# A fourth block of the up projection through seven products, with its sums, transposes and combinations moved

## The chip, the cores and the metric

The kernel runs on one core of one Trainium2 chip. The metric is the device time of one execution in microseconds (us), the median of several runs. Lower is better. Inputs, weights and the result are float32 in the chip's main memory, and the products must hold nearly float32 accuracy.

## The reference

One residual block over 256 tokens of width 2048: a mixer (retention and latent attention, merged by gates, then `w_out`), and behind it an MLP with a squared ReLU. The change lies in the last two lines of the loop and in the seam to them.

```python
def reference(x, ...):
    h = x
    u = _rmsnorm(h, norm_mix_g[l])
    h = h + _mixer(u, ...)                      # ends in merged @ w_out
    z = _rmsnorm(h, norm_mlp_g[l]) @ w_up[l]    # (256 x 2048) @ (2048 x 8192)
    h = h + jnp.square(jax.nn.relu(z)) @ w_down[l]
    return _rmsnorm(h, norm_f_g)
```

## The kernel before, in words

**Splitting.** Every float32 operand is split into two parts, `hi` (ScalarE casts, L550) and `lo` (VectorE subtracts, L551), and a product of two operands is three matmuls: hi by hi, hi by lo, lo by hi. So each weight tile of 128 x 1024 that a DMA brings into a `raw` buffer costs one ScalarE cast and one VectorE subtraction before TensorE can use it. There are five `raw` buffers, and seven pairs of `hi` and `lo` in this stage (four, and three named `more`).

**The MLP's up projection** has 8192 columns. It is computed in two ways.

- *Units* (`Unit`, L1264): 128 columns at a time, in two halves of 8 contraction tiles. A half is 8 matmuls of 512 columns (the weight's `hi` against both parts of the tokens, L176) and 8 of 256 columns (`lo`, L180), into one PSUM bank `z`. At the end ScalarE copies the bank out (L1291), VectorE adds its two halves (L1292), ScalarE applies ReLU and the square, and GpSimd's queue stores the result to the array `hid`.
- *Steps* (`Step`, L287): 1024 columns, a *block*, at a time, as a 2 x 2 block product with seven block products in place of eight. A block takes eight steps, one for each 256 rows of the contraction. A step is four parts with 2, 2, 2 and 1 products, 21 matmuls of 512 columns (L333 to L335) into seven PSUM banks `zs`, one for each product. Of the chip's eight banks one is left for `z` or for transposes. A step's weights come by two DMAs of 512 KB (`sraw` and `raw`), and VectorE forms their sums `forms` (L307, L316, L317) before these are split like other weights.

The tokens' side of the seven products needs combinations of token blocks, `hc` (`combine`, L221). One call of `make` makes those of a quarter of the contraction, that is of two steps, and holds two `raw` buffers while it does.

When a block's last step is done, `s_end` (L515) combines the seven banks into the block's four quarters in the tile `zo`. These have tokens in the partitions, but the down projection wants columns there, so four *turns* (`turn`, L1302) transpose them on TensorE, four 128 x 128 transposes each into a bank `zt`, and ScalarE squares and GpSimd stores.

**The order** in this stage is written by hand. `stream` (L470) walks a list of *parts* (a part of a step, or half a unit). At part n it issues the loads up to part n+6, the preparation (split, sums) up to part n+4, then the matmuls of part n; then `soon` (L463) issues what was put in the list `later` with a delay counted in parts. The instructions of each engine run in just this order, and each engine waits in place.

In the list stand three early units, then the blocks with units between their parts, then two late units. Before the change there are three blocks and 40 units. 35 units stand inside: one behind the last part of each step but the last, and one behind the second part of every other step. A turn stands ahead of the second part of steps 1 to 4 of the next block; the last block's turns stand with the late units.

```python
            for f, i, o in PRODUCTS:               # L329
                if i == part:
                    ...
                    PE.matmul(q, ah, hi[:, o], start=first, stop=False)
                    PE.matmul(q, al, hi[:, o], start=False, stop=False)
                    PE.matmul(q, ah, lo[:, o], start=False, stop=last)
```

**The seam.** Ahead of the stage, `wo` (the product with `w_out`, L1233) runs over four column blocks, with tokens transposed (L1224) one block later. The first two quarters of `hc` are made beside its second and third column blocks; quarters three and four are made in the stage, from parts 7 and 24 on, a piece every second part. Behind the stage, the down projection `dn` (L357 to L359) reads `hid` back and uses products of the same two kinds; it is not edited, but takes the pairs of columns in the order of units first, then blocks.

Of the kernel before, what the change touches and what calls it, by code (L numbers as in the profile page):

```python
# [13 lines left out]
F32R = mybir.dt.float32r  # L14
# [3 lines left out]
ALU = mybir.AluOpType  # L18

P = 128  # L20
S = 256
D = 2048
KT = D // P
# [4 lines left out]
CHUNK = 64  # L28
DFF = 8192
FT = DFF // P  # L30
SU = 3
SJ = KT // 2
ST = SU * 1024 // P
EARLY, LATE = 3, 2
AHEAD = 4
PAIRED = 6
# [69 lines left out]
def block_kernel(ctx: ExitStack, tc: tile.TileContext, A):  # L106
# [9 lines left out]
    def big(name, dt=F32, shape=(P, KT, S)):  # L116
        return act.tile(list(shape), dt, tag="act16", name=name)
# [127 lines left out]
    class Combos:  # L245
# [4 lines left out]
            self.name, self.pair, self.t = name, pair, []  # L250

        def make(self, c):
            if c % 2 == 0:
                self.t.append(big(f"{self.name}{c // 2}", F32R, (P, KT // 4, 2, 4, P)))
            return combine(self.pair, 2 * c, self.t[-1][:, c % 2 * 2 : c % 2 * 2 + 2])

        def get(self, f, j):
# [29 lines left out]
    class Step:  # L287
# [32 lines left out]
            pass  # L320

        def mm(self, part):
            if part == 0 and self.j == 0:
                self.qs.update({f: (mmps if f in (3, 4, 2, 5) else atps)(f"zs{uid[0]}{f}") for f in (3, 4, 2, 5, 6, 1, 7)})
            if part == 1:
                self.between()
            hi, lo = self.ws.pop(part)
            first, last = self.j == 0, self.j == SJ - 1
            for f, i, o in PRODUCTS:  # L329
                if i == part:  # L330
                    ah, al = self.x.get(f, self.j)
                    q = self.qs[f]
# [3 lines that stand above are left out]
            if part == 3 and last:  # L336
                self.end()
# [123 lines left out]
    later = []  # L461
# [5 lines left out]
                later.remove(entry)  # L467
                entry[1]()

    def stream(parts, after):  # L470
        loaded = prepped = 0
        for n, (it, h) in enumerate(parts):
            ahead = AHEAD if n else 2
            while loaded < min(len(parts), n + ahead + 3):
# [37 lines left out]
            st.after = last  # L512
        return parts

    def s_end(qs, out, tmp):  # L515
# [3 lines left out]
        def tt(eng, o, a, b, op=ALU.add):  # L519
            eng.tensor_tensor(out=o, in0=a, in1=b, op=op)  # L520

        SC.copy(t3, qs[3])
        tt(V, e, qs[6], t3)
        SC.copy(q5, qs[5])
        tt(V, f, qs[2], e, ALU.subtract)
        SC.copy(c12, qs[1])
        tt(V, c21, qs[4], f)
        SC.copy(c22, qs[7])
        tt(V, c11, q5, f)
        yield  # L530
        tt(V, e, e, q5, ALU.subtract)
        yield
        tt(V, c12, c12, e)
        yield
        tt(V, c22, c22, t3)
        yield

    def join(out, ps):
# [689 lines left out]
                split(hT.hi(kt), hT.lo(kt), pT[:, j * S : (j + 1) * S], scale=g)  # L1228
    zp = ctx.enter_context(tc.tile_pool(name="zp", bufs=1))
    hidd = ctx.enter_context(tc.tile_pool(name="hidd", bufs=1, space=bass.MemoryType.DRAM))  # L1230
    hc = Combos("hc", hT)
# [32 lines left out]
    class Unit:  # L1264
# [23 lines left out]
        def evict(self):  # L1288
            pair, n = divmod(ST + self.i, 2)
            t = zp.tile([P, 2, S], F32, tag="hs", bufs=5, name=f"hs{pair}{n}")  # L1290
            SC.copy(t, self.ps.rearrange("p (j n) -> p j n", j=2))  # L1291
            V.tensor_tensor(out=t[:, 0], in0=t[:, 0], in1=t[:, 1], op=ALU.add)  # L1292
# [18 lines left out]

    def step(u, j, qs):
        def end():
            sums = s_end(qs, zo[:, 0].rearrange("p (t c) n -> p t c n", t=2), zo[:, 1])
# [19 lines left out]
    slots = [(u, j, h) for u in range(SU) for j in range(SJ) for h in (1, 3)][:-1]  # L1334
    whole = [t for t in slots if t[2] == 3]
    room = len(units) - len(whole)
    halves = [t for t in slots if t[2] == 1]
    if room >= 0:
        use = set(whole) | {halves[i * len(halves) // room] for i in range(room)}
    else:  # L1340
        use = {t for t in whole if t[1] != PAIRED or t[0] >= -room}
    for u in range(SU):
        qs = {}
        for j in range(SJ):
# [8 lines left out]
        un = Unit(i, 0, drain(((0, 1), (1, 2))[n]))  # L1353
        parts += [(un, 0), (un, 1)]

    hp = ctx.enter_context(tc.tile_pool(name="hp", bufs=1))
    combs, sets = {}, {}
    ssf = cp.tile([P, 2, SSF], F32, name="ssf")
    rf = cp.tile([P, 2], F32, name="rf")
# [126 lines left out]
    def after(n):  # L1486
        nonlocal making, zo, keep, hn2, gt
        if n == 0:
            mlp_turn(3)
            keep = hidd.tile([P, 2, D], F32, name="hnkeep")  # L1490
            SC.dma_start(keep, hn)
            zo = big("zo", shape=(P, 2, 4, 512))
        elif n in MAKE:
            making = hc.make(2 + MAKE.index(n))
        if n < 2 * EARLY or n % 2 == 0:
            next(making, None)
        if hooks.get(n) == 0:
# [4 lines left out]
        elif hooks.get(n) == 1:  # L1502
            for t in range(2):
                for c in range(2):
# [3 lines left out]
                    later.append([2 * t + c, one])  # L1508
                    later.append([6 + 2 * t + c, lambda t=t, c=c: scale(t, c)])

    zo = keep = hn2 = gt = None
    rings(zp, MORE, True, forms)
    with tc.manual_schedule(engines=MANUAL):
        stream(parts, after)
        assert not later
        for t in range(2):
            for c in range(2):
# [98 lines left out]
```

## Time and profile before

| What | Value |
|---|---|
| median of 3 runs | 1564.05 us (1563.8 to 1564.08) |
| the profiled execution | 1564.87 us |
| its span, first to last instruction | 1563.1 us |
| granted TensorE clock, mean | 0.998 |
| up projection, first `z` to first `dn` matmul | 876 to 1221 us |
| down projection | 1221 to 1563 us |

The page of the profile gives for each engine the time in which it was busy. PE is TensorE with its matmuls, PEld its weight loads, DVE VectorE, ACT ScalarE, POOL GpSimd, SP the engine whose queue issues the loads. A matmul's duration in the rows is its latency; matmuls are pipelined, and one follows the other sooner than that. What a stretch of work takes is therefore read from starts, or from the chain of waits, in which each piece stands with the time that the path spent in it.

### The profile page before, as it was taken

The numbers are of one execution on the slowest core, as the hardware profiler recorded it, in microseconds if no ns is written. First come the engines' busy times: TensorE is split into PE (matmuls) and PEld (weight loads), VectorE is DVE, ScalarE is ACT, GpSimd is POOL, SyncE is SP. The second block draws the span as 40 slices with busy tenths as digits, with TensorE's granted clock in tenths as the row PEclk, the third lists the DMA queues.
The fourth block names the chain that finished last, engine by engine and source line by source line (L and its number), as shares of the span: only waits on it lengthen the run. The fifth ranks groups of instructions, "written<-read, shape, count | busy, mean of one in ns | idle before, by whom it ended". The sixth has DMA issues, their size and how long they took to land.

```text
span 1563.1 us, 21388 instructions
## 1 busy us (share of the span) xinstructions
PE 1550.3 (99%) x7655; PEld 1310.8 (84%) x7655; DVE 1317.3 (84%) x1787; ACT 962.8 (62%) x1416; POOL 39.1 (3%) x76
## 2 busy tenths in 40 slices
PE   9999999999999999999999999999999999999997
PEld 7888888888898888888888888888888888888886
DVE  7998877899977988976566698887978899989996
ACT  7546555566545667874445566676767766656664
POOL 0000000000000000000000000000000100000000
PEclk9999999999999999999999999999999999999999
DMA  8666755466656664445556657676675977686773
GB/s 328 208 202 208 234 163 160 154 202 211 203 170 222 207 197 149 158 127 164 191 197 217 234 193 252 210 229 229 212 247 190 375 269 240 235 308 210 265 256 115
DMA packets 107626, 333.70 MB, mean 213 GB/s; under 512 B 11264, under 2 KB 12160, under 8 KB 106496
## 3 DMA queue, kind: packets, MB, share of 16 engines
q1 hardware_dynamic: 104208, 318.71, 61.3%
q0 software_dynamic: 3168, 11.54, 1.8%
q10 hardware_dynamic: 144, 2.10, 0.4%
q8 instruction: 60, 0.98, 0.2%
q14 instruction: 46, 0.38, 0.1%
HBM read 319.72 MB, written 12.58 MB: 213 GB/s over the span
## 4 chain that ended last, share of the span: by engine, by line
PE 78%; DVE 2%; issue 1%; ACT 1%; DMA 0%; DVEq 0%; POOLq 0%; POOL 0%; ACTq 0%
PE z L176 9%; PE dn L359 7%; PE dn L358 7%; PE dn L357 7%; PE z L180 5%; PE zs L335 2%; PE zs L333 2%; PE zs L334 2%; PE mo L214 2%; PE mo L215 2%; PE mo L217 2%; PE wo L214 2%; PE wo L215 2%; PE wo L217 2%; PE gm L357 2%; PE yr L358 2%
## 5 line engine op out<-in xcount | busy, mean ns | idle before, releaser
L169 DVE TENSOR_TENSOR lo<-raw,hi 128x1024 fp32r<-128x1024 f32 (+1 forms) x148 | 173.2, 1172 | 90.9 <-ACT hi L168 90.8
L551 DVE TENSOR_TENSOR lo<-raw,hi 128x1024 fp32r<-128x1024 f32 (+3 forms) x214 | 232.1, 1101 | 20.1 <-ACT hi L550 19.6
L168 ACT CAST hi<-raw 128x1024 fp32r<-128x1024 f32 (+1 forms) x148 | 149.6, 1012 | 156.0 <-PE mo L215 44.9
L550 ACT CAST hi<-raw 128x1024 fp32r<-128x1024 f32 (+3 forms) x214 | 199.9, 953 | 51.6 <-issue 7.9
L551 DVE TENSOR_TENSOR morelo<-raw,morehi 128x1024 fp32r<-128x1024 f32 (+1 forms) x118 | 127.1, 1098 | 19.0 <-ACT morehi L550 18.5
L550 ACT CAST morehi<-raw 128x1024 fp32r<-128x1024 f32 (+1 forms) x118 | 109.1, 949 | 10.7 <-PE dn L359 2.9
L550 ACT CAST hi<-forms 128x1024 fp32r<-128x1024 f32 x70 | 73.7, 1052 | 51.8 <-DVE forms L307 26.3
L176 PE MATMUL z<-hT,morehi 128*128 128x512 f32 x408 | 101.6, 391 | 0.0
L357 PE MATMUL dn<-hi,dd 128*128 128x512 f32 x230 | 89.6, 389 | 0.0
L359 PE MATMUL dn<-hi,dd 128*128 128x512 f32 x230 | 89.5, 389 | 0.0
L358 PE MATMUL dn<-lo,dd 128*128 128x512 f32 x230 | 89.5, 389 | 0.0
L551 DVE TENSOR_TENSOR lo<-forms,hi 128x1024 fp32r<-128x1024 f32 x70 | 85.0, 1220 | 5.3 <-ACT hi L550 4.9
L176 PEld LDWEIGHTS z<-hT,morehi 128*128 128x128 f32 x408 | 74.9, 188 | 14.4
L1291 ACT COPY hs<-z 128x512 f32<-128x512 f32 x40 | 23.5, 587 | 70.6 <-PE z L180 70.6
L357 PE MATMUL dn<-morehi,dd 128*128 128x512 f32 x156 | 60.7, 389 | 0.0
L358 PE MATMUL dn<-morelo,dd 128*128 128x512 f32 x156 | 60.7, 389 | 0.0
L359 PE MATMUL dn<-morehi,dd 128*128 128x512 f32 x156 | 60.7, 389 | 0.0
L180 PEld LDWEIGHTS z<-hT,morelo 128*128 128x128 f32 x408 | 55.6, 190 | 4.0
L176 PE MATMUL z<-hT,hi 128*128 128x512 f32 x232 | 57.9, 392 | 0.0
L307 DVE TENSOR_TENSOR forms<-raw,sraw 128x1024 f32<-128x1024 f32 x46 | 56.1, 1219 | 1.1 <-DMA raw<-w_up_s 1.1
L180 PE MATMUL z<-hT,morelo 128*128 128x256 f32 x408 | 56.9, 282 | 0.0
L358 PEld LDWEIGHTS dn<-lo,dd 128*128 128x128 f32 x230 | 43.2, 188 | 9.0
(500 smaller groups left out, 4195.1 us busy)
## 6 DMA issues: line engine op xcount, KB each, us to landing
raw<-w_down SPq DMA_DIRECT2D x106, 512.0 KB, 6.1
raw<-w_up SPq DMA_DIRECT2D x80, 512.0 KB, 4.9
raw<-w_rv SPq DMA_DIRECT2D x32, 512.0 KB, 4.9
raw<-w_rg SPq DMA_DIRECT2D x32, 512.0 KB, 4.0
raw<-w_gret SPq DMA_DIRECT2D x32, 512.0 KB, 4.4
raw<-w_ret_o SPq DMA_DIRECT2D x32, 512.0 KB, 5.0
raw<-w_gmla SPq DMA_DIRECT2D x32, 512.0 KB, 4.3
raw<-w_mla_o SPq DMA_DIRECT2D x32, 512.0 KB, 3.7
```

Source lines behind the costliest of these rows:

```text
L168: SC.copy(hi, raw)
L169: V.tensor_tensor(out=lo, in0=raw, in1=hi.bitcast(F32), op=ALU.subtract)
L176: PE.matmul(out, w[0][:, k], x.both(k0 + k), start=start and k == 0, stop=False)
L180: PE.matmul(out[:, :S], w[1][:, k], x.hi(k0 + k), start=False, stop=stop and k == n - 1)
L214: PE.matmul(out, x.hi(k0 + k, ts), w[0][:, k], start=start and k == 0, stop=False)
L215: PE.matmul(out, x.lo(k0 + k, ts), w[0][:, k], start=False, stop=False)
L217: PE.matmul(out, x.hi(k0 + k, ts), w[1][:, k], start=False, stop=stop and k == nk - 1)
L357: PE.matmul(q, ah, wh, start=start, stop=False)
L358: PE.matmul(q, ah, wl, start=False, stop=False)
L359: PE.matmul(q, al, wh, start=False, stop=self.left[f] == 0)
L550: SC.copy(hi, val)
L551: V.tensor_tensor(out=lo, in0=val, in1=hi.bitcast(F32), op=ALU.subtract)
```

## The change

It has five parts.

1. `SU` goes from 3 to 4: four blocks, so half of the up projection, go through seven products, and 32 units are left of 40. Of the 27 inside, six stand behind the second part of the steps 0, 1, 2, 3, 5 and 6 of each block (`MIDST`), and one behind the last step of each block but the last.
2. `s_end`: ScalarE copies all seven banks to `zo` at the block's end, in three groups over two parts; VectorE's seven sums read the copies and are spread over the parts of the next block (`SUMS`). The last block keeps the old way.
3. A turn stands ahead of the first part of steps 2, 3, 5 and 6 (`TURN`), two parts ahead of the unit in that step.
4. The third quarter of `hc` is made beside the fourth column block of `wo`. The first half of `hc` moves to a memory of its own, `zx`, which the down projection's tiles take over later.
5. The addition of a unit's halves (L1292 before) is put one part later, what follows it also.

```diff
-SU = 3
+SU = 4
-MAKE = 7, 2 * EARLY + 18
-SUMS = (4, 7, 10), (0, 1, 2)
+MAKE = 7
+SUMS = (0, 1, 2, 5, 8, 11, 13, 15, 17), (0, 1, 2)
+TURN = 2, 3, 5, 6
+MIDST = 0, 1, 2, 3, 5, 6
...
         def mm(self, part):
+            if part == 0:
+                self.between()
...
-            if part == 1:
-                self.between()
...
+        else:
+            for group in (((t3, 3), (c21, 4)), ((f, 2), (q5, 5)), ((e, 6), (c12, 1), (c22, 7))):
+                for o, n in group:
+                    SC.copy(o, qs[n])
+                yield
+            tt(e, e, t3)
+            yield
+            tt(f, f, e, ALU.subtract)
+            yield
+            tt(c21, c21, f)
+            yield
+            tt(c11, q5, f)
+            yield
+        tt(e, e, q5, ALU.subtract)
         yield
...
-        if c in (1, 2):
+        if c:
             for _ in hc.make(c - 1):
                 pass
...
-            V.tensor_tensor(out=t[:, 0], in0=t[:, 0], in1=t[:, 1], op=ALU.add)
...
-            later.append([2, rest])
+            later.append([1, lambda: V.tensor_tensor(out=t[:, 0], in0=t[:, 0], in1=t[:, 1], op=ALU.add)])
+            later.append([3, rest])
...
-            if turns and j:
+            if turns and j in TURN:
                 turns.pop(0)()
...
+    use = {(u, j, 1) for u in range(SU) for j in MIDST} | {(u, SJ - 1, 3) for u in range(SU - 1)}
```

**TensorE around the second block's first turn, before.** `zs` is the block's matmuls, `z` a unit's, `zt` the transposes; `hi` and `lo` are split weights, `hT` the tokens, `hc` their combinations.

```order
L180 MATMUL z_9425<-hT_7391,morelo_69_9373 128x256 x8
L333 MATMUL zs_9318<-hi_9396,hT_7390 128x512
L334 MATMUL zs_9318<-hi_9396,hT_7390 128x512
L335 MATMUL zs_9318<-lo_9397,hT_7390 128x512
L333 MATMUL zs_9319<-hi_9396,hc_7713 128x512
L334 MATMUL zs_9319<-hi_9396,hc_7713 128x512
L335 MATMUL zs_9319<-lo_9397,hc_7713 128x512
L1309 MATMUL zt_9486<-con,zo 128x128 x4
L333 MATMUL zs_9320<-hi_9409,hc_7713 128x512
```

The same place after the change:

```order
L181 MATMUL z_9197<-hT_7391,morelo_61_9154 128x256 x8
L336 MATMUL zs_9068<-morehi_62_9165,hc_7716 128x512
L337 MATMUL zs_9068<-morehi_62_9165,hc_7716 128x512
L338 MATMUL zs_9068<-morelo_62_9166,hc_7716 128x512
L336 MATMUL zs_9069<-morehi_62_9165,hT_7390 128x512
L337 MATMUL zs_9069<-morehi_62_9165,hT_7390 128x512
L338 MATMUL zs_9069<-morelo_62_9166,hT_7390 128x512
L336 MATMUL zs_9070<-hi_9178,hT_7390 128x512
L337 MATMUL zs_9070<-hi_9178,hT_7390 128x512
L338 MATMUL zs_9070<-lo_9179,hT_7390 128x512
L1329 MATMUL zt_9266<-con,zo 128x128 x4
L336 MATMUL zs_9064<-hi_9191,hT_7390 128x512
```

Before, every step ended with a unit, so between a unit and the turn stood one part of six matmuls. Now the unit stands in the middle of the step before, nine matmuls lie between, and the turn heads its step.

**ScalarE at the end of the first block, before.** `COPY zo<-zs` reads a block's bank, `COPY hs<-z` a unit's, the casts prepare the parts that follow.

```order
L550 CAST morehi_62_9239<-sraw_9210 128x1024
L550 CAST hi_9253<-forms 128x1024
L522 COPY zo<-zs_8317 128x512
L524 COPY zo<-zs_8320 128x512
L526 COPY zo<-zs_8322 128x512
L528 COPY zo<-zs_8323 128x512
L550 CAST hi_9268<-raw_9236 128x1024
L550 CAST hi_9289<-raw_9251 128x1024
L1291 COPY hs_9309<-z_9272 128x512
```

And after the change:

```order
L568 CAST morehi_53_8998<-forms 128x1024
L539 COPY zo<-zs_8325 128x512
L539 COPY zo<-zs_8326 128x512
L539 COPY zo<-zs_8327 128x512
L539 COPY zo<-zs_8328 128x512
L568 CAST morehi_54_9009<-raw_8981 128x1024
L539 COPY zo<-zs_8329 128x512
L539 COPY zo<-zs_8330 128x512
L539 COPY zo<-zs_8331 128x512
L568 CAST morehi_55_9033<-raw_8996 128x1024
L1311 COPY hs_9053<-z_9013 128x512
```

Three copies more stand ahead of the second cast; the three VectorE operations that read banks directly (L520, `zo<-zs`) are gone from that engine's order at this place.

More of the change, by code (lines that the diff above doesn't have):

```diff
@@ L468, in soon, with stream @@
                 entry[1]()
-    def stream(parts, after):
+    def stream(parts, after, before=lambda n: None):
         loaded = prepped = 0
@@ L473, in stream @@
             ahead = AHEAD if n else 2
+            before(n)
             while loaded < min(len(parts), n + ahead + 3):
@@ L513, in product, with s_end, tt @@
         return parts
-    def s_end(qs, out, tmp):
+    def s_end(qs, out, tmp, last):
         t3, e, f, q5 = (tmp[:, i] for i in range(4))
         c11, c12, c21, c22 = (out[:, t, c] for t in range(2) for c in range(2))
[L519 to L529, printed above, removed]
+        def tt(o, a, b, op=ALU.add):
+            V.tensor_tensor(out=o, in0=a, in1=b, op=op)
+        if last:
+            SC.copy(t3, qs[3])
+            tt(e, qs[6], t3)
+            SC.copy(q5, qs[5])
+            tt(f, qs[2], e, ALU.subtract)
+            SC.copy(c12, qs[1])
+            tt(c21, qs[4], f)
+            SC.copy(c22, qs[7])
+            tt(c11, q5, f)
[11 more added lines that the diff above has]
+            yield
+            tt(c11, q5, f)
+            yield
+        tt(e, e, q5, ALU.subtract)
         yield
-        tt(V, e, e, q5, ALU.subtract)
+        tt(c12, c12, e)
         yield
-        tt(V, c12, c12, e)
-        yield
-        tt(V, c22, c22, t3)
+        tt(c22, c22, t3)
         yield
@@ L1509, in after, with before @@
                     later.append([6 + 2 * t + c, lambda t=t, c=c: scale(t, c)])
+    hp = None
     zo = keep = hn2 = gt = None
     rings(zp, MORE, True, forms)
+    def before(n):
+        nonlocal hp
+        if hp is None and n + AHEAD + 3 >= reach:
+            zctx.close()
+            hp = ctx.enter_context(tc.tile_pool(name="hp", bufs=1))
     with tc.manual_schedule(engines=MANUAL):
-        stream(parts, after)
+        stream(parts, after, before)
         assert not later
```

25 lines of the change are left out of this document (10 added, 15 removed).

## The prediction

> **What bounds the kernel now.** I read the page first, then the waits of TensorE, then the up projection alone.
>
> ```profile
> PE 1550.3 (99%) x7655; PEld 1310.8 (84%) x7655; DVE 1317.3 (84%) x1787; ACT 962.8 (62%) x1416; POOL 39.1 (3%) x76
> ```
>
> A busy PE need not be a PE at its pace, so the second view asks what TensorE ever waited for. These are all the rows it has (us in total, times, longest):
>
> ```profile
> PE spin L573 <- DVE cold L570: 1.2, 1, 1.2
> PE ms L1047 <- DVE k L541: 1.0, 1, 1.0
> PE my L584 <- DVE pp L551: 0.7, 1, 0.7
> PE first L652 <- DVE x L554: 0.6, 1, 0.6
> ```
>
> 3.5 us in 1563.1, none in the two MLP stages. The busy times of the stretch from the first `z` to the first `dn` matmul (PE, PEld, DVE, ACT, POOL, clock, DMA share, GB/s) say the same:
>
> ```profile
> 876.00:1221.00 345.00, 344.93 (x1844) 297.29 (x1843) 291.21 (x334) 236.54 (x338) 26.12 (x48) 1.00 0.67 225
> ```
>
> TensorE is full there, VectorE 84% and ScalarE 69% busy. If that holds, a change here is worth exactly the TensorE time that it takes out. What the pieces take is read from the chain of waits, whose pieces are the path's own time (start, us, what); only the first and last row of a piece is shown.
>
> ```profile
> 957.23 1.81 PE z L176 x8
> ...
> 961.83 0.95 PE z L180 x8
> ...
> 967.57 1.81 PE z L176 x8
> ...
> 972.18 0.95 PE z L180 x8
> ...
> 975.88 1.81 PE z L176 x8
> ...
> 980.49 0.95 PE z L180 x8
> ...
> 983.51 1.81 PE z L176 x8
> ...
> 1014.39 0.95 PE z L180 x8
> ...
> 1020.63 1.81 PE z L176 x8
> ...
> 1025.23 0.95 PE z L180 x8
> ...
> 1029.41 1.81 PE z L176 x8
> ```
>
> A unit runs from 957.23 to 961.83 + 0.95 = 962.78: **5.55 us**. What lies between two units is steps: 962.78 to 967.57 is a whole step, 21 matmuls, **4.79**. A step that a unit splits takes 973.13 to 975.88 and 981.44 to 983.51, 2.75 + 2.07 = **4.82**. With one turn inside, a whole step takes 1015.34 to 1020.63 = 5.29, half a step 1026.18 to 1029.41 = 3.23: a turn costs 0.50 and 0.48, say **0.49**.
>
> One place in the stage runs unevenly:
>
> ```profile
> 947.92 0.39 PE L334 MATMUL zs<-hi,hc 128*128 128x512 f32 x1
> 948.38 0.50 PE L335 MATMUL zs<-lo,hc 128*128 128x512 f32 x1
> 948.72 0.39 PE L333 MATMUL zs<-hi,hc 128*128 128x512 f32 x1
> ```
>
> Starts are 0.46 and 0.34 apart where 0.23 is the rule: **0.34 us** lost, too short for the list of waits.
>
> The Trainium skill ("Perfetto Trace Analysis", Identifying the Most-Contended Engine) calls matmul busy time a bad measure and wants the weight loads' share instead. By that TensorE would be 84% used, level with VectorE, and less TensorE work need buy nothing. The rows above speak against it here: equal pieces repeat to 0.03 us, and nothing is waited for.
>
> **The change part by part.** *Work on TensorE.* Eight units go: 8 x 5.55 = 44.4 us out. Steps were 24, half of them split by a unit; now they are 32, of which six in every eight are split: 24 x 4.82 + 8 x 4.79 - 12 x 4.82 - 12 x 4.79 = 38.68 us in. Four more turns: 4 x 0.49 = 1.96 in. Sum: -3.76 us. All of it lies on the path.
>
> *The turn's price* has its own row:
>
> ```profile
> L1309 PE MATMUL zt<-con,zo x48: 270/272/273, 1016.6 to 1220.6; 128*128 128x128 f32 x48
> ```
>
> 0.27 is one transpose's latency; four together cost 0.49 as above, 0.12 each. The Trainium skill ("TensorE: Matmul & The Clock Gate", Part 4) gives about 275 ns for one transpose in a kernel. As an estimate from that page, 16 more would cost 4.4 us. The row's 272 ns agrees with the figure as a latency, and the two turns measured above show that it isn't the pace.
>
> *Third combination beside wo.* It is two VectorE operations of 1024 and four of 256 columns, 2 x 1.22 + 4 x 0.42 = 4.1 us by the rows below, and one ScalarE cast of 1.05. It leaves the parts 24 to 30, right ahead of the place where the 0.34 us was lost, and goes to the last column block of wo, between these VectorE rows:
>
> ```profile
> 868.85 1.23 DVE L551 TENSOR_TENSOR lo<-raw,hi 128x1024 fp32r<-128x1024 f32 x1 [1.49 <-ACT hi L550]
> 871.57 1.22 DVE L551 TENSOR_TENSOR lo<-raw,hi 128x1024 fp32r<-128x1024 f32 x1 [1.49 <-ACT hi L550]
> 874.24 1.23 DVE L551 TENSOR_TENSOR lo<-raw,hi 128x1024 fp32r<-128x1024 f32 x1 [1.45 <-ACT hi L550]
> ```
>
> 4.4 us of idle before three splits, and the combinations of blocks 1 and 2 already run so beside wo without a wait of TensorE. So nothing in wo; uncovered, it would be at most 4.1 us. It holds two `raw` tiles, and the early units' loads stand behind them on SP. One load lands in
>
> ```profile
> raw<-w_up SPq DMA_DIRECT2D x80, 512.0 KB, 4.9
> ```
>
> 4.9 us; the one that waits for the combination (second half of unit 0) can go at about 869, lands at 874, and its matmuls come three half units behind 876, at 884. Nothing. I take the 0.34 us as gained, since its likeliest cause leaves; bounds 0 and 0.34. The sum is -3.76 - 0.34 = **-4.1 us**.
>
> *Block sums from copies.* Reading SBUF instead of PSUM does not change a VectorE operation (count, min/median/max ns):
>
> ```profile
> L520 DVE TENSOR_TENSOR zo<-zo x12: 681/684/686, 999.7 to 1216.8; 128x512 f32<-128x512 f32 x12
> L520 DVE TENSOR_TENSOR zo<-zs,zo x9: 684/691/692, 997.7 to 1211.2; 128x512 f32<-128x512 f32 x9
> L522 ACT COPY zo<-zs x3: 574/575/579, 995.2 to 1208.3; 128x512 f32<-128x512 f32 x3
> ```
>
> ScalarE does seven copies where it did four: 7 x 0.58 = 4.1 us. Behind them in its queue stand the casts of the next step; ahead of the next block's first matmul, which needs the first copied bank, TensorE has a unit of 5.55 us. Nothing on the path, but it idles VectorE, which waits for those casts.
>
> *VectorE* must keep pace. Its order through a step and a unit:
>
> ```profile
> 966.67 1.22 DVE L307 TENSOR_TENSOR forms<-raw,sraw 128x1024 f32<-128x1024 f32 x1
> 967.81 1.22 DVE L551 TENSOR_TENSOR morelo<-sraw,morehi 128x1024 fp32r<-128x1024 f32 x1
> 968.94 0.68 DVE L316 TENSOR_TENSOR forms<-forms,sraw 128x512 f32<-128x512 f32 x1
> 969.66 0.69 DVE L317 TENSOR_TENSOR forms<-forms,raw 128x512 f32<-128x512 f32 x1
> 970.27 1.22 DVE L551 TENSOR_TENSOR lo<-forms,hi 128x1024 fp32r<-128x1024 f32 x1
> 971.40 2.35 DVE L551 TENSOR_TENSOR lo<-raw,hi 128x1024 fp32r<-128x1024 f32 x2
> 973.79 0.42 DVE L1292 TENSOR_TENSOR hs<-hs 128x256 f32<-128x256 f32 x1
> 974.74 1.23 DVE L551 TENSOR_TENSOR lo<-forms,hi 128x1024 fp32r<-128x1024 f32 x1 [0.53 <-ACT hi L550]
> 975.88 0.69 DVE L551 TENSOR_TENSOR morelo<-raw,morehi 128x512 fp32r<-128x512 f32 x1
> ...
> 982.10 0.43 DVE L1292 TENSOR_TENSOR hs<-hs 128x256 f32<-128x256 f32 x1 [2.77 <-ACT hs L1291]
> ```
>
> A step: 966.67 to 971.40 is 4.73, and 1.14 + 0.69: 6.56 us. A unit: 2.35 + 0.42 = 2.77. Seven block sums: 7 x 0.69 = 4.8. A block has now 8 steps and 7 units: 8 x 6.56 + 7 x 2.77 + 4.8 = 76.7 us on VectorE. On TensorE it has 6 x 4.82 + 2 x 4.79 + 7 x 5.55 + 4 x 0.49 = 79.3. So 97%, where the old mix (8 steps, 11.7 units) gives 89.7 to 105.2, 85%, which the row of the whole stage bears out. It still fits.
>
> *Moved turns and additions.* The addition after a unit (L1292) stands one part later, so VectorE may run one part further ahead: nothing on a full TensorE. A turn takes the one bank that is left, which the copy of the unit before it must free (first rival): it stood one part of six matmuls, 1.4 us, behind that unit, and now stands nine, 2.07. The next unit takes the bank two parts, 2.75, after the turn. The pool for the down projection's tiles now waits for the last reader of the first combinations, 24 parts earlier: nothing.
>
> The profiled execution took 1564.87 us, span 1563.1; 1564.87 - 4.1 = 1560.8 there. The median shown is 0.82 us lower: 1564.05 - 4.1 = **1559.9**.
>
> **The rivals.** *1. The bank is not free for the turn.* Two ScalarE rows:
>
> ```profile
> 957.41 1.05 ACT L550 CAST hi<-forms 128x1024 fp32r<-128x1024 f32 x1 [0.68 <-DVE forms L307]
> ...
> 973.17 0.59 ACT L1291 COPY hs<-z 128x512 f32<-128x512 f32 x1 [2.24 <-PE z L180]
> ```
>
> Ahead of the copy in the queue stands a cast that needs VectorE's sums. Normally the copy starts with the unit's end, as in the second row, and is done 0.6 later, 1.5 before the turn. If VectorE is late as in the first row, 0.68 + 1.05 + 0.59 = 2.32 us pass, 0.25 more than the 2.07. At all twelve turns inside blocks that is 3.0 us: 1562.9, no change. For it: VectorE at 97%. Against: until now the turn had only 1.4 us, and nothing was lost there.
>
> *2. VectorE becomes the bound: slower.* Two steps of each block (the fifth and the eighth) have no unit inside: 6.56 us of VectorE beside 4.79 of TensorE, short by 1.77. Without a lead that is 8 x 1.77 = 14.2 us, 1564.05 - 4.1 + 14.2 = 1574.1. The lead: when the fourth step's unit ends, VectorE has to do 0.59 + 0.42 (copy, addition), 0.69, and 1.14 + 1.14 for the sixth step, 3.98 us, and TensorE wants that after 2.07 + 4.79 = 6.86. So it decides from 2.9 us of lateness at that point. For it: only 2.6 us a block are spare, and 4.1 us of copies hold VectorE's inputs up. Against: the lead is regained with every split step (10.37 on TensorE, 9.33 on VectorE).
>
> *3. Late loads.* Denser steps ask for their `raw` tiles closer together. If a loss of the size seen, 0.34 us, came at each of the eight whole steps, where loads follow closest, it is 2.7 us: 1562.6, no change. For it: the lost 0.34 came after parts in which a combination held two of five tiles, and one such stretch stays. Against: DMA share 0.67.
>
> *4. TensorE is not the bound*, though always busy: with 297.29 us of weight loads in 345, 14% would be room, and the saved matmuls buy nothing: 1564.05, no change. Against: no piece is ever stretched except at 948. *5. Transposes at full latency:* a turn of 4 x 0.272 = 1.09 us is 0.60 over 0.49, at four new turns 2.4 us: 1562.4, no change. The old turns don't cost that. The change does do what it says: the built order has 672 `zs` matmuls for 504 and 1024 `z` for 1280.
>
> **How the numbers follow.** Forecast 0.70, third rival 0.12, second 0.08, first 0.06, fourth 0.03, fifth 0.01. The forecast's own range: pieces repeat to 0.03 us, and some twenty (units, steps, turns) differ, so 0.6 below, 1559.3; above it ends where a gain can't be told, 1560.9. A measurement of this kernel can tell about 0.2%, 3.1 us, from no change: faster is below 1560.9, slower above 1567.2. Faster 0.70, same 0.22, slower 0.08. For 8 in 10 the range goes from 1559.3 to 1562.6, which takes in the third and fifth rivals, and the first where it holds at ten turns of twelve or fewer.
>
> **What would show it.** Right: the up projection takes 341 us for 345; units and steps keep 5.55 and 4.79 or 4.82; VectorE's share of that stretch is 92% or more; no gap over 0.3 us among `zs` matmuls. First rival: gaps ahead of `zt`. Second: gaps inside the fifth and eighth steps, with VectorE never idle. Third: VectorE's sums waiting for `w_up_s`. The forecast is wrong if the stretch shrinks by less than 3 us.

## The result and the profile after

The changed kernel takes 1559.82 us (median of 8 runs, 1559.43 to 1560.54), the kernel before 1564.07 beside it (8 runs, 1563.72 to 1565.18). The ratio is 0.9972, 95% interval 0.9961 to 0.9983: **4.25 us faster**. The forecast was 1559.9, or -4.1. The profiled execution took 1560.36 us, span 1558.6, 4.5 less than the one before.

The engines' line of the page, the waits of TensorE, and the up projection's row (PE, PEld, DVE, ACT, POOL, clock, DMA share, GB/s), all of the kernel after:

```profile
PE 1545.9 (99%) x7583; PEld 1304.4 (84%) x7583; DVE 1347.5 (86%) x1826; ACT 976.9 (63%) x1429; POOL 37.1 (2%) x72
```

```profile
PE spin L591 <- DVE cold L588: 1.2, 1, 1.2
PE ms L1065 <- DVE k L559: 1.0, 1, 1.0
PE my L602 <- DVE pp L569: 0.7, 1, 0.7
PE first L670 <- ACT hi L568: 0.5, 2, 0.3
```

```profile
876.00:1217.00 341.00, 341.00 (x1774) 291.51 (x1773) 317.99 (x366) 249.23 (x351) 24.05 (x44) 1.00 0.69 230
```

TensorE still waits nowhere in the MLP. VectorE went from 84% of the stage to 318 of 341 us, 93% (forecast: 92% or more). The first `z` matmul starts at 876.23, 0.10 later than before, and the first `dn` matmul at 1216.08 for 1220.61. So the stage takes 339.86 us for 344.48, **4.63 less**, and nothing else moved by more than 0.1.

Where the 4.63 come from is seen when the distances between the starts of neighbouring matmuls are added up by the tile that the first of the two writes:

```
            before              after               difference
z           1280 in 222.74      1024 in 178.27      -44.47
zs           504 in 116.62       672 in 155.05      +38.43
zt            48 in   4.34        64 in   5.75       +1.41
ht             8 in   0.79         8 in   0.79        0
stage               344.48              339.86       -4.63
```

The chain of waits after, around a fifth step (start, us, what):

```profile
1006.38 1.81 PE z L177 x8
...
1010.99 0.95 PE z L181 x8
...
1018.77 0.44 PE zt L1329 x4
...
1021.98 1.81 PE z L177 x8
```

The unit takes 1006.38 to 1011.94, 5.56 us as before. Up to the next unit lie 10.04 us: the second half of the fourth step, the whole fifth, the first half of the sixth, 42 `zs` matmuls and a turn.

One prediction of the profile did not come true. The stall of 0.34 us at 948 was to go. It went, and two others came, at 916 and 942 (rows of the timeline, two places of the first block):

```profile
916.15 0.39 PE L337 MATMUL zs<-morehi,hc 128*128 128x512 f32 x1
916.46 0.50 PE L338 MATMUL zs<-morelo,hc 128*128 128x512 f32 x1
916.80 0.39 PE L336 MATMUL zs<-morehi,hc 128*128 128x512 f32 x1
...
941.82 0.39 PE L337 MATMUL zs<-hi,hc 128*128 128x512 f32 x1
942.13 0.50 PE L338 MATMUL zs<-lo,hc 128*128 128x512 f32 x1
942.47 0.39 PE L336 MATMUL zs<-hi,hc 128*128 128x512 f32 x1
```

0.31 + 0.34 where 0.46 is the rule, twice: 0.4 us in all. Each time the late operand is a `lo`, VectorE's product. At 916 VectorE itself had waited for a load of `w_up_s`, from 909.83 to 910.45, and before the change it had done so from 941.26 to 942.36, six microseconds ahead of the stall at 948. These are its only waits for a load in the stage (VectorE's waits, first row before, second after; us in total, times, longest):

```profile
DVE forms L307 <- DMA raw<-w_up_s: 1.1, 1, 1.1
DVE forms L310 <- DMA raw<-w_up_s: 0.6, 1, 0.6
```

That is the sign which the prediction gave for its third rival, late loads, and both times a combination was being made, which holds two of the five `raw` tiles. In kernels 3 and 12 below neither the wait nor the stall at 916 appears, while the one at 942 does. So the stall at 916 goes with a late load, and the one at 942 is VectorE's own.

How near to its limit VectorE runs in the other blocks too is seen where a TensorE instruction is set beside the end of what it needs. The rows are VectorE's and TensorE's timelines in the second block:

```profile
990.90 0.68 DVE L524 TENSOR_TENSOR zo<-zo 128x512 f32<-128x512 f32 x1
...
1013.55 1.23 DVE L569 TENSOR_TENSOR lo<-forms,hi 128x1024 fp32r<-128x1024 f32 x1 [0.86 <-ACT hi L568]
...
1019.23 1.22 DVE L569 TENSOR_TENSOR morelo<-forms,morehi 128x1024 fp32r<-128x1024 f32 x1
```

```profile
992.19 0.60 PE L1329 MATMUL zt<-con,zo 128*128 128x128 f32 x4
...
1020.90 0.40 PE L338 MATMUL zs<-morelo,hc 128*128 128x512 f32 x1
```

Two places of a block have little to spare. The first turn needs block sums that end at 990.90 + 0.68 = 991.58, **0.61 us** ahead of it; the second part of the sixth step needs a `morelo` that ends at 1020.45, **0.45 us** ahead. The prediction's rival of a late VectorE worked with 2.9 us. So the next question was what had kept the kernel on the right side of so small a margin.

### The profile page after: what moved, and what is told of

Read it like the earlier page. It is cut to its first block, busy times and chain, and to the rows that moved or that the text cites. A ratio compares the mean times of both kernels' runs of the same rounds, so it can differ in the third digit from the quotient of the medians.

```text
span 1558.6 us, 21305 instructions
## 1 busy us (share of the span) xinstructions
PE 1545.9 (99%) x7583; PEld 1304.4 (84%) x7583; DVE 1347.5 (86%) x1826; ACT 976.9 (63%) x1429; POOL 37.1 (2%) x72
## 4 chain that ended last, share of the span: by engine, by line
PE 79%; DVE 1%; issue 1%; ACT 1%; DVEq 0%; POOLq 0%; POOL 0%; ACTq 0%
PE z L177 8%; PE dn L360 7%; PE dn L361 7%; PE dn L362 7%; PE z L181 4%; PE zs L336 3%; PE zs L338 3%; PE zs L337 3%; PE mo L216 2%; PE mo L215 2%; PE mo L218 2%; PE wo L216 2%; PE wo L215 2%; PE wo L218 2%; PE gm L362 2%; PE gm L360 2%
## 5 line engine op out<-in xcount | busy, mean ns | idle before, releaser
L569 DVE TENSOR_TENSOR lo<-raw,hi 128x1024 fp32r<-128x1024 f32 (+3 forms) x237 | 253.8, 1084 | 28.7 <-ACT hi L568 28.1
L568 ACT CAST hi<-raw 128x1024 fp32r<-128x1024 f32 (+3 forms) x237 | 218.9, 940 | 57.8 <-PE yr L362 6.9
L569 DVE TENSOR_TENSOR morelo<-raw,morehi 128x1024 fp32r<-128x1024 f32 (+1 forms) x87 | 93.3, 1085 | 4.7 <-ACT morehi L568 4.7
L568 ACT CAST morehi<-raw 128x1024 fp32r<-128x1024 f32 (+1 forms) x87 | 80.4, 943 | 5.7 <-issue 2.1
L568 ACT CAST morehi<-forms 128x1024 fp32r<-128x1024 f32 x50 | 52.8, 1055 | 49.6 <-DVE forms L310 30.2
L177 PE MATMUL z<-hT,hi 128*128 128x512 f32 x296 | 74.0, 392 | 0.0
L569 DVE TENSOR_TENSOR morelo<-forms,morehi 128x1024 fp32r<-128x1024 f32 x50 | 61.0, 1220 | 4.0 <-ACT morehi L568 3.5
L177 PEld LDWEIGHTS z<-hT,hi 128*128 128x128 f32 x296 | 54.2, 188 | 10.4
L177 PE MATMUL z<-hT,morehi 128*128 128x512 f32 x216 | 53.7, 391 | 0.0
L362 PEld LDWEIGHTS dn<-hi,dd 128*128 128x128 f32 x240 | 45.1, 188 | 9.4
L360 PEld LDWEIGHTS dn<-hi,dd 128*128 128x128 f32 x240 | 45.1, 188 | 9.4
```

Source lines behind the costliest of these rows:

```text
L177: PE.matmul(out, w[0][:, k], x.both(k0 + k), start=start and k == 0, stop=False)
L360: PE.matmul(q, ah, wh, start=start, stop=False)
L362: PE.matmul(q, al, wh, start=False, stop=self.left[f] == 0)
L568: SC.copy(hi, val)
L569: V.tensor_tensor(out=lo, in0=val, in1=hi.bitcast(F32), op=ALU.subtract)
```

## The experiments

Two theories. **A**, the prediction's: TensorE's own work sets the time, and the parts moved cost and bring nothing. **B**: the parts moved are what lets the saved work show; without them a TensorE that is always ready waits for VectorE and ScalarE. Where the expectations speak of a theory V, it is B for VectorE alone: its lead at the narrow places counts, not its share of busy time. Twelve kernels were timed, each in five rounds against the kernel before; ratios are to it. "Stage" is the time from the first `z` to the first `dn` matmul in the profiled execution (before 344.48, after 339.86).

**1. The fourth block alone.** The kernel before with

```diff
-SU = 3
+SU = 4
```

> The kernel before with only the count of seven-product blocks raised from 3 to 4; sums, turns, additions and combinations stay as they were. Theory A (the time follows TensorE's own work, the rest is hidden): TensorE does what it does in the changed kernel, so about 1559.8, no more than 0.5 above. Theory B (the moved parts are what lets the saved work show): the old order, with a VectorE that is 93% busy, loses time at the sums, which take 4 banks straight from PSUM while the next block wants them, at the turns and where the two late combinations fall: several gaps of 0.3 to 1 us among the zs matmuls at every change of block and at 900 to 950, 1562 or more.

Measured: 1568.4 us, ratio 1.0025 (1.0015 to 1.0035), stage 348.65. The same 8 units are gone, and it is **slower** than before, 8.8 us of stage behind the changed kernel. (With four blocks the old rule puts every unit inside at a step's end and none in a step's middle.) Waits of TensorE:

```profile
PE zs L335 <- DVE morelo L551: 2.4, 3, 1.9
PE zt L1309 <- ACT hs L1291: 2.1, 3, 0.7
```

The second row is the prediction's first rival, in the old place of the turn. ScalarE's timeline at the first of these three turns, which starts at 988.22:

```profile
986.11 1.05 ACT L550 CAST morehi<-forms 128x1024 fp32r<-128x1024 f32 x1 [1.41 <-PE z L180]
987.07 0.61 ACT L550 CAST morehi<-raw 128x512 fp32r<-128x512 f32 x1
987.59 0.58 ACT L1291 COPY hs<-z 128x512 f32<-128x512 f32 x1
```

TensorE goes on from the unit at 985.95; the unit's copy stands behind two casts, and the bank is free at 988.17. Theory A falls here: without the moves the whole gain is lost, and more. The longest stall, 1.9 us at 916, follows a wait of VectorE of 1.71 us for a load of `w_up_s`, again while a combination was being made.

**2. The rest alone.** The changed kernel with three blocks and the old places of the units:

```diff
-SU = 4
+SU = 3
...
-    use = {(u, j, 1) for u in range(SU) for j in MIDST} | {(u, SJ - 1, 3) for u in range(SU - 1)}
+    slots = [(u, j, h) for u in range(SU) for j in range(SJ) for h in (1, 3)][:-1]
...
+    use = set(whole) | {halves[i * len(halves) // room] for i in range(room)}
```

> The changed kernel with three seven-product blocks, and the units placed as before: sums from copies, turns two parts ahead, additions later, third combination beside wo, but TensorE's work as before. Theory A: 1563.7 to 1564.1, as the kernel before, less the 0.34 us that was lost at 948 where the third combination left. Theory B: the moved parts are worth something by themselves; with VectorE at 84% there is little to gain, so at most 0.5 below, and more than 0.5 below would mean that part of the gain is theirs. Up projection 344 to 344.5 us.

Measured: 1570.76 us, ratio 1.0040 (1.0027 to 1.0054), stage 350.80. Neither theory had it. The waits name one cause:

```profile
PE zt L1329 <- ACT hs L1311: 5.4, 8, 0.7
```

The old rule puts a unit at a step's end, the new turn stands at a step's beginning: eight turns come directly behind a unit and wait for its copy. The distance from `z` to `zt` there is 0.96 us for the usual 0.12, 8 x 0.84 = 6.7 us, in a stage that is 6.3 longer (the stall of 0.34 us at 948 is gone here too, and `zs` is broken less often). So the new place of the turn is worth nothing by itself; place of turn and place of unit are one decision. What the other moves are worth with three blocks this run does not tell.

**3. The old block sums.**

```diff
-SUMS = (0, 1, 2, 5, 8, 11, 13, 15, 17), (0, 1, 2)
+SUMS = (4, 7, 10), (0, 1, 2)
...
-        if last:
+        if True:
```

> The changed kernel with the block sums made as before (four copies, three sums from PSUM at once, then three over parts 4, 7 and 10). Theory A: 1559.8 to 1560.3, since a unit of 5.55 us stands between two blocks and the reads cost VectorE the same. Theory B: in a block's first step VectorE has the sums in one lump of 4 x 0.69 us ahead of the step's own sums, and no lead (the narrowest part had 0.46 us): 1 to 2 us lost at each of three changes of block, 1562.8 to 1566.

Measured: 1559.5 us, ratio 0.9969 (0.9958 to 0.9981), stage 339.64 for 339.86. Theory A is right here: the block sums from copies bring nothing in the changed kernel, and the shorter old way does as well.

**4. The third combination back in the stage.**

```diff
-MAKE = 7
+MAKE = 7, 24
...
-        if c:
+        if c in (1, 2):
```

> The changed kernel with the third combination back in the up projection, from part 24 on. Theory A: 4.1 us more of VectorE work in a stretch whose steps have units; a loss of the size seen before, 0.34 us, at most: 1559.8 to 1560.2. Theory B: VectorE had no lead in the first block of the changed kernel, where gaps of 0.2 us showed at 916 and 942, so 4.1 us more, and two held raw tiles, come out nearly whole: 1562 to 1564.

Measured: 1563.09 us, ratio 0.9992 (0.9983 to 1.0), stage 343.76, 3.9 more than the changed kernel's; B's number. One long stall shows in the timeline (first row: what idle time ended), and the two stretches behind it by windows:

```profile
944.48 0.58 PE L338 MATMUL zs<-lo,hc 128*128 128x512 f32 x1 [1.94 <-DVE lo L569]
```

```profile
942.00:944.50 2.50, 0.56 (x4) 0.13 (x2) 2.50 (x4) 2.47 (x4) 0.00 (x0) 1.00 0.96 321
944.50:948.20 3.70, 3.70 (x9) 2.95 (x10) 3.70 (x4) 0.77 (x1) 0.00 (x0) 0.54 0.69 218
948.20:952.00 3.80, 3.80 (x23) 3.31 (x22) 3.77 (x6) 1.05 (x1) 0.00 (x0) 1.00 0.94 277
```

VectorE is busy for all of the first 2.50 us, of which TensorE stands idle 1.94. Then TensorE's granted clock is 0.54 for 3.7 us, and matmuls start 0.427 us apart for 0.228: eight of them, 8 x 0.2 = 1.6 us more. The 4.1 us of VectorE work come out as 2.75 us of waiting (by the starts; 0.5 of it in a shorter gap at 940) and 1.6 us of slow clock, less the 0.4 us of gaps that the changed kernel has in the first block.

**5. The turn late.** Each turn directly ahead of a step's second part, as in the kernel before:

```diff
-            if part == 0:
-                self.between()
...
+            if part == 1:
+                self.between()
```

> The changed kernel with each turn directly ahead of a step's second part instead of its first, so nearer to the next unit. Theory A: no change, 1559.6 to 1560.1: the turn's bank was free in both kernels. Rival: the unit after the turn takes the bank that the turn's copy must free; that margin was 0.49 us with the turn in its new place and the move takes three matmuls, 0.7 us, off it, so 0.2 to 0.3 us are lost at each of the twelve turns inside blocks that a unit follows: 1562 to 1563, with gaps ahead of z.

Measured: 1566.91 us, ratio 1.0015 (1.0006 to 1.0023), stage 346.84, 7.0 more than the changed kernel. The rival's mechanism, but 2 to 3 times its size. The units that follow a turn start late: in each of three blocks one by 1.4 us, two by 0.2 and one by 0.1, and behind every such gap the next matmul is 0.1 late. ScalarE's timeline at the first:

```profile
992.68 1.06 ACT L568 CAST morehi<-forms 128x1024 fp32r<-128x1024 f32 x1
994.85 0.42 ACT L1314 ACTIVATE hs<-hs 128x256 f32<-128x256 f32 x1 [1.11 <-DVE hs L1317]
995.30 0.42 ACT L1276 ACTIVATE hs<-hs 128x256 f32<-128x256 f32 x1
995.62 0.60 ACT L568 CAST morehi<-raw 128x512 fp32r<-128x512 f32 x1
996.13 0.59 ACT L1281 ACTIVATE hs<-zt 128x512 f32<-128x512 f32 x1
```

The last row frees the turn's bank. Ahead of it ScalarE stands 1.11 us still, for the addition of the unit before, which this change moved one part later.

**6. The same with the addition early.** To part the two, kernel 5 with the addition back behind the copy:

```diff
             SC.copy(t, self.ps.rearrange("p (j n) -> p j n", j=2))
+            V.tensor_tensor(out=t[:, 0], in0=t[:, 0], in1=t[:, 1], op=ALU.add)
...
-            later.append([1, lambda: V.tensor_tensor(out=t[:, 0], in0=t[:, 0], in1=t[:, 1], op=ALU.add)])
-            later.append([3, rest])
+            later.append([2, rest])
```

> The changed kernel with the turn directly ahead of the second part and the addition of a unit's halves directly behind its copy, as the kernel before had them. With the turn alone moved back, three first turns cost 1.4 us each and the others 0.2 to 0.3. Theory Q (ScalarE's queue: the turn's copy stood behind an activation that waited for the late addition): the three 1.64 gaps shrink to 0.42 or less, so 1567 less 3 x 1.2 = 1563 or better. Theory D (distance alone: a turn six matmuls ahead of a unit is too near whatever the additions do): 1566 to 1567 as before the addition was put back.

Measured: 1563.45 us, ratio 0.9996 (0.9987 to 1.0004), stage 343.00. From the last matmul ahead of such a unit to the unit's first, kernel 5 had three distances of 1.64 us and six of 0.42, where 0.23 is the rule. The 1.64 became 0.65, not 0.42; the 0.42 stayed. The activation no longer waits for VectorE:

```profile
992.76 0.42 ACT L1315 ACTIVATE hs<-hs 128x256 f32<-128x256 f32 x1
...
994.99 0.59 ACT L1281 ACTIVATE hs<-zt 128x512 f32<-128x512 f32 x1
```

So of the 7.0 us, 3.8 are the pair of a late addition and a late turn, and 3.1 are the distance alone: six matmuls between turn and unit are too few for ScalarE's queue here, twelve are enough. Turn and addition both in their old places, with the rest as changed, is this kernel: 3.1 us of stage. The early addition with the turn in its new place was not run, so what the addition's move does there is not shown.

**7 and 8. More VectorE work.** One or two (`k`) additions of 512 columns at the end of every step's sums, into a tile that nothing reads:

```diff
+                if env["sraw"]:
+                    for _ in range(k):
+                        V.tensor_tensor(out=idle[:, :512], in0=self.fa[:, 0, :512], in1=self.fa[:, 1, :512], op=ALU.add)
```

> The changed kernel with one more VectorE addition of 512 columns (0.69 us, into a tile that nothing reads) at the end of each seven-product step: 32 x 0.69 = 22 us more of VectorE in a stage where it idles 23 us of 341. Theory A (VectorE keeps pace and the spare counts as a whole): up to 1 us lost, 1559.8 to 1560.9. Theory V (the lead counts, not the share): the narrowest parts, the first of every sixth step, have 0.46 us to spare and come right behind two steps without much room, so 2 x 0.69 - 0.46 = 0.9 us or more is lost in each block, plus the whole of it in the first block where there was no lead, 8 x 0.69 = 5.5: 1563 to 1569.

> The changed kernel with two such VectorE additions per seven-product step, into a tile that nothing reads: 44 us more, where 23 are idle. Both theories: at least 44 - 23 = 21 us slower, 1581 or more, with VectorE gapless; theory V, which has some of the idle time unusable, gives up to 44, 1604. The slope from one addition to two tells how near to the bound VectorE stands: 22 us for the second if it is wholly the bound by then.

Measured: 1572.28 us with one (ratio 1.0046, 1.0033 to 1.0059), 1607.81 with two (1.0277, 1.0263 to 1.0291). The edit reached further than meant: 22 seven-product steps of the down projection took the additions too, 54 in all and not 32. So only the stage is used: 347.04 and 366.65, 7.2 and 26.8 more than the changed kernel. The first 22 us cost 7.2 where 23 were idle, the second 19.6. Its waits in the stage, with one addition:

```profile
PE zs L341 <- DVE morelo L572: 1.9, 3, 0.7
PE zs L341 <- DVE lo L572: 1.7, 2, 1.0
PE zt L1333 <- DVE zo L527: 0.7, 1, 0.7
```

Two further rows, of 0.6 each, put waits of `zt` down to casts; they are the first turns of the other two blocks. The waits lie at 916 and 942 in the first block, and in the others at the first turn and in the sixth step: the places of the small margins. The share of busy time says that there is room for all of it; the margins say that there isn't.

**9 and 10. Where the VectorE work lies.** Twelve additions, 8.3 us, in blocks 2 to 4, either in the fifth and sixth step of each or in the second and third:

```diff
+                if type(self) is Step and self.u and self.j in (4, 5):
+                    for _ in range(2):
```

```diff
+                if type(self) is Step and self.u and self.j in (1, 2):
+                    for _ in range(2):
```

> The changed kernel with two extra VectorE additions of 512 columns (0.69 us each, into a tile that nothing reads) in the fifth and in the sixth step of blocks 1 to 3: 12 additions, 8.3 us, of the 23 idle. The fifth step holds no unit, and the first part of the sixth had 0.46 us to spare. Theory A (share): nothing, 1559.8 to 1560.3. Theory V (the lead at the narrow place counts): 3 x (4 x 0.69 - 0.46) = 6.9 us lost there, 1566.7, and up to 1.7 each more where a stall of 2 us is followed by matmuls at half clock.

> The same 12 extra additions, 8.3 us, but in the second and the third step of blocks 1 to 3, which hold units and are followed by one more that does. Theory A: nothing. Theory V: VectorE waits for other engines in these steps, so most of it goes into that time; what is left at the narrow place is at most a third, 0 to 2 us, 1559.8 to 1562. As much as in the fifth and sixth steps would say that the sum of VectorE's work counts and not where it lies.

Measured: 1563.97 us (ratio 0.9998, 0.9989 to 1.0007) and 1566.21 (1.0012, 1.0003 to 1.0021); stages 343.82 and 346.29. The order is the opposite of what theory V said: the steps that hold units cost more. Each kernel has three stalls, one in each block; the first of each (timelines of TensorE):

```profile
1021.89 0.50 PE L341 MATMUL zs<-morelo,hc 128*128 128x512 f32 x1 [1.11 <-DVE morelo L572]
```

```profile
994.14 0.63 PE L1333 MATMUL zt<-con,zo 128*128 128x128 f32 x4 [1.73 <-ACT morehi L571]
```

The second stands at the block's first turn. Its releaser is not the cast that the row names, which belongs to another tile. VectorE's timeline has it: the block sum that the turn reads stands directly behind the last two of the four additions and ends at 993.99.

```profile
991.98 1.41 DVE L323 TENSOR_TENSOR idle<-forms 128x512 f32<-128x512 f32 x2
993.31 0.68 DVE L527 TENSOR_TENSOR zo<-zo 128x512 f32<-128x512 f32 x1
```

By the margins: 2.76 us of additions ahead of each place, less 0.61 at the first turn, make 2.15; the turn came 1.89 late (2.12 where 0.23 is the rule). Less 0.45 in the sixth step, they make 2.31; the matmul came 1.27 late, because VectorE had 0.86 us of idle time in between to fill (the row at 1013.55 above). So what an addition costs is set by the next narrow place behind it. My place for the absorbing steps was wrong: they lie ahead of one that I had not counted.

**11. A fifth block.**

```diff
-SU = 4
+SU = 5
...
-MIDST = 0, 1, 2, 3, 5, 6
+MIDST = 1, 3, 5
```

> The changed kernel with a fifth seven-product block (five blocks of eight steps; 24 units, inside the second, fourth and sixth steps and at the ends of blocks). Theory A (only TensorE counts): another 4.6 us off, 1555.2. Theory V (VectorE is the bound): its work in the up projection goes from 318.0 to 318.0 + 8 x 6.56 - 8 x 2.77 + 4.8 = 353 us, more than TensorE's 335; with no idle time 1573, at the 98.8% that VectorE reached with two extra additions a step 1577, with the 23 us that it idles now 1596. So slower than before.

Measured: 1586.58 us, ratio 1.0145 (1.0130 to 1.0159), stage 363.32. VectorE is busy 350.67 of 362 us:

```profile
PE zt L1329 <- DVE zo L524: 12.0, 4, 3.0
PE zs L338 <- DVE lo L569: 4.9, 5, 1.1
PE zs L338 <- DVE morelo L569: 4.4, 6, 1.3
```

The prediction's second rival, one block later: 353 us of VectorE work don't fit into the 335 that TensorE has, and TensorE waits 21 us, 12 of them at the first turns of the blocks. The time lies in the middle of theory V's range. With the work ordered like this, four blocks is where the exchange ends.

**12. Every transpose twice.** The same transpose issued twice, to the same place:

```diff
-                PE.transpose(pT[:, o : o + P], src, ident)
+                for _ in range(2):
+                    PE.transpose(pT[:, o : o + P], src, ident)
```

> The changed kernel with every transpose of the sixteen turns issued twice, to the same place: 64 more. By the pace read from the starts (four transposes with their surroundings 0.45 us, one behind another 0.088): 64 x 0.088 = 5.6 us, 1565.5; the upper end, by a whole turn's price of 0.45, 16 x 0.45 = 7.2, 1567. By the latency of 0.272 us for each: 17.4 us, 1577.2. The Trainium skill (TensorE: Matmul & The Clock Gate, Part 4) gives about 275 ns for a transpose; an estimate from it is 17.6 us.

Measured: 1566.79 us, ratio 1.0015 (1.0006 to 1.0024), stage 346.32, 6.5 more than the changed kernel. The chain has the turn at

```profile
992.09 0.88 PE zt L1330 x8
```

0.88 for eight transposes, where four take 0.44: 0.109 for each by the starts, and 64 x 0.109 = 7.0. The stage is only 6.5 longer because its `zs` matmuls take 0.5 less; the stall at 916, 0.2, is a part of that. Each row of a transpose still says 0.27. The 275 ns of the Trainium skill ("TensorE: Matmul & The Clock Gate", Part 4) agree with that latency and would have made 17.6 us; the pace is what a full TensorE pays. My 0.088 was a mean over four distances of a turn, three of 0.109 from transpose to transpose and one of 0.028 to the next matmul; the transposes themselves stand 0.109 apart.

## Why the prediction was right, and where its steps were not

The mechanism was right: on a TensorE that never waits, a unit less is 5.55 us less and a step more is about 4.8 us more. `z` gave 44.47 for the 44.4 of the sum. The total, -4.1 for a measured -4.25 (-4.6 in the stage of the profiled execution), is nearer than its terms, because two of them missed in opposite directions, and that is luck:

- *Steps* (booked at +38.68) came at about +37.9. Inside an unbroken run the `zs` matmuls start 0.227 us apart, and each run costs 0.027 more, once. Two lengths of run show it: 21 matmuls take 4.79 and 30 take 6.83, where 21 + 9 apart take 4.79 + 2.07 = 6.86. So 168 more matmuls are 38.1, and as units now break `zs` into 28 runs for 36, 0.2 goes off. The prediction booked +0.36 for twelve more steps that are split in the middle, and forgot that a unit at a step's end breaks the run as well.
- *The stall at 948* (-0.34) was taken as gone for its likeliest cause, the combination. It did go, and in kernel 2, which also makes the third combination beside `wo`, it is gone too. But two other stalls of together 0.4 us came, so the term is about +0.1.
- *Turns* held: a run with a turn in it takes 0.47 to 0.49 more, in both kernels, 1.92 for the booked 1.96.

Together: -44.47 + 37.9 + 1.92 + 0.07 = -4.6, the stage's number.

*"Moved turns and additions: nothing", "third combination: nothing", "block sums: nothing on the path".* As prices of the new places these held: but for the two gaps in the first block, no wait appears in the stage. But I did not ask what the old places would have cost with the fourth block. It is 3.9 us of stage for the combination (kernel 4), 3.1 for turn and addition together (kernel 6) and 7.0 for the turn alone, with the addition late (kernel 5), where the whole gain is 4.6; only the sums are free in both forms. And alone the fourth block is slower than before (kernel 1). That the gain needs the new places of the combination and of the turn was not in the forecast, and a reader could have dropped one on its word.

*The first rival's argument against itself* failed: "until now the turn had only 1.4 us, and nothing was lost there". That was with a VectorE busy 84% of the stage. With the fourth block in the old order the bank is late at three turns (kernel 1).

*VectorE at 97%* was estimated for a block; from the second block's first turn to the third's VectorE is busy 74.5 of 79.1 us, 94%, and 93% over the stage. The conclusion that it still fits held. The lead of 2.9 us did not: the two narrow places have 0.61 and 0.45. The ledger took the fourth step's end as the start and counted only work still to be done from there, as if VectorE were in step with TensorE at that point; it is behind. "The lead is regained with every split step" fell with kernel 10: 8.3 us of additions in such steps cost 6.4.

*The third rival* (late loads) put its losses at the eight whole steps. There they did not come: behind the first block the three runs of 42 matmuls and a turn, each with a whole fifth step in it, take 10.04 us every time, and all four runs of 30, each with a whole eighth step, 6.83. What there was of late loads is the 0.2 us at 916.

*The fourth rival* (TensorE not the bound, 84% of weight loads) is excluded by the result: eight units less bought all of their 5.56 us each. *The fifth* (a transpose at its latency) is excluded by the turns, 0.47 to 0.49 us for the 1.09 that it needs, and by kernel 12.

Open stays what the moved parts are worth with three blocks, since kernel 2 mixed them with a bad place of the units; what the new places of the units and of the addition bring by themselves with four blocks; and how much the old block sums, free in kernel 3, are of what kernel 1 loses. Kernel 1's trace points to a part: in the first step of blocks 2 to 4, at 978, 1059 and 1139, TensorE comes 0.3 to 0.5 us late for a `lo` that VectorE makes directly behind four block sums.

## What to carry to other kernels

When the bound engine is full, price an exchange on it by start-to-start pieces, then list for each edit what the place it leaves would cost after the exchange, not only what the new place costs. For an engine that follows at 90% and more, its share says little: look for the instruction whose operand ends last ahead of it, in every period of the loop, and take that margin as the room. A PSUM bank that two users share is freed by the queue of the engine that empties it, so its users' places and that queue's order have to be chosen together.

## What the hardware showed that was not expected

A stall can cost more than its length. In kernel 4 and in kernel 1 TensorE idled 1.9 us, and within a microsecond its matmuls started 0.427 us apart for 3.4 us, at a granted clock of 0.54 in kernel 4's row above. It does not follow every stall: of eleven idle times between 1.85 and 3.1 us in kernels 1, 4, 8 and 11, five were followed by it, and the four longest, of 3.0 us in kernel 11, were not; there it came once behind a stall of 1.3 us. The Trainium skill ("TensorE: Matmul & The Clock Gate", Part 1) says that the array falls to half clock after an idle window of about 3.4 us, and that the window runs freely; the pace of 0.427 and the length of 3.4 us agree with it, while here less than 2 us of idle time was enough.

The traces' records of the granted clock show where the stalls fell. Every slow stretch in the stage is 3.41 us long, and in kernel 8 the three begin 85.33 us apart, 25 such lengths. If time is cut into cells of that length from there, the five idle times had 1.93 us or more in the one cell just ahead of the slow one. The other six were cut by a boundary, with at most 1.92 in one cell. The stretch behind the stall of 1.3 us doesn't fit: its cell had 1.5 us of idle time, less than others that stayed fast. So where a stall falls in the cells seems to count beside its length. This was read from the traces afterwards, and no run moved a stall to try it.
